# A one-core kernel of three mixer layers: refitted durations, the shared port of two engines, and overwriting transfers in the planner that sets the order of issue

## The chip, the core and the metric

The kernel runs on one core of a Trainium2 chip. A core has five instruction streams: PE (matrix products, with its weight loads as PEld), DVE (VectorE), ACT (ScalarE), POOL (GpSimd) and SP, which here only issues transfers. Each stream works in its own order; semaphores tie them together. The metric is the device time of one execution in microseconds, the median of several runs.

## The reference

Input x is 512 tokens by 1024, all in float32. Two blocks follow each other; the first has an even and an odd layer, the second has one layer. Each layer is a projection of 1024 columns into many, several kinds of attention, a gate, and a projection back.

```python
# first block, two layers
mod = cond @ w_ada[layer] + b_ada[layer]          # cond = silu(c), one row: a matrix-vector product
shift, scale, gate = jnp.split(mod, 3, axis=-1)
h = rmsnorm(x, g_pre[layer]) * (1.0 + scale[:, None, :]) + shift[:, None, :]
...
    y = even_mixer(h, ...)     # z = h @ w_in; MLA attention and sliding-window attention; silu gate; @ w_out
...
    y = odd_mixer(h, ...)      # differential attention and forgetting attention; silu gate; @ w_out
x = x + gate[:, None, :] * rmsnorm(y, g_post[layer])

# second block, one layer
h = x @ w_in
o_nsa = nsa_mixer(...)             # compressed, selected and window attention, gated
o_sb = stick_breaking_mixer(...)
o_hg = hgrn2_mixer(...)            # a gated linear recurrence in chunks of 64
x = layer_norm(ALPHA * x + mixed @ w_out, ln_g, ln_b)
```

## The kernel before, in words

Every float32 product is made of three fp32r products: a value is split into a high part (a cast) and a low part (value less high part). For a weight tile of 128 by 1024 this is `wload`: the transfer into `wraw` (L107), the cast into `whir` on ACT (L109) and the subtraction into `wlor` on DVE or POOL (L113); PE then runs high by high, high by low and low by high (`mm`, L80). Activations are split by `split` (L90 on ACT or L94 on DVE for the high part, L95 on DVE for the low part). `wraw`, `whi` and `wlo` have few buffers each, so a weight's transfer starts when an older one has been split.

The row `mod` is a matrix-vector product of 24 weight tiles a layer (of 128 by 1024 each). It is done on DVE: `gemv_acc` multiplies a tile by a column of `cond` and adds it to a sum `sa` (L175 for the first of eight, L177 for the others). These tiles come through one buffer, `graw` (transfer L157), so the next transfer waits for the step on the tile before. In the first layer the first sums take their tiles through `V` and `og` instead (L660), and the first sum is kept in `pthr`; the inputs x come into `Pr` (L648) and the unit matrix into `ident` (L76), which PE needs for its transposes (L140).

In attention, L367 (`dup`) copies key and query rows between partition halves by transfers inside the core's memory (32 or 64 rows by 512); L383 on DVE adds the mask and takes the row's extreme, L385 on ACT takes the exponential, L395 on POOL normalises, PE transposes (L140), L94 or L90 and L95 split the result.

The code writes instructions in a plain order. At its end `Plan(tc).pin()` gives each of the five engines a fixed order: `duration` gives each instruction a time, a time in which it holds its engine, and a third number (for PE the share of activity, for transfers the bytes); `edges` collects what must wait for what; `schedule` is a list scheduler that walks a model of the five engines, and takes on each engine the ready instruction with the best rank (the place in the plain order, mixed with the longest path that hangs on it, weight `PATH`); `pin` fixes the order that comes out. The real waits are those of the data and of the buffers; the plan only says in which order an engine comes to them. An engine that stands at an instruction whose data isn't there does nothing else.

In the names of rows a number behind a name (`graw_472`) is the instance; in rows of the trace these numbers are left out.

Of the kernel before, what the change touches and what calls it, by code (L numbers as in the profile page):

```python
# [1780 lines left out]
class Plan:  # L1781
# [4 lines left out]

    ENGINES = {"PE": 0, "DVE": 1, "Activation": 2, "Pool": 3, "SP": 4}
    LATENCY = (55, 35, 35, 35, 35)
    BYTES_PER_NS, DMA_LATENCY, LANES = 330.0, 1700.0, 8
    QUANTUM, QUIET, TABLE = 3413.0, 0.6, 1283  # L1790
    PATH = 0.10

    def __init__(self, tc):
        self.tc = tc
# [34 lines left out]
        return t, p0, p1, self.masks[key]  # L1829


    def duration(self, x, e):
        kind = type(x).__name__[4:]
        aps = lambda l: [a.bass_ap for a in l if getattr(a, "bass_ap", None) is not None]
        free = lambda ap: math.prod(int(c) for _, c in list(ap.ap)[1:])
        psum = lambda ap: "PSUM" in str(getattr(ap.tensor, "space", ""))
        I, O = aps(x.ins), aps(x.outs)
        if e == 0:
            n, m = free(I[0]), free(I[1])
            w = 108 if m > 64 else 60  # L1840
            if x.is_transpose:
                return 275, 112, 0
            if "float32r" in str(x.ins[0].dtype):
                n = max(n / 2.26, w if m > 32 else 50)
                return n + 163, n, n
            w = 2 * max(2 * n / 2.26, w if m > 32 else 30)
            return w + 163, w, 4 * n / 2.26 if n > 8 else 0
        if kind == "DMACopy":
            b = 4 * math.prod(int(c) for _, c in O[0].ap)
            return 0, 550 if b <= 140000 else 330, b  # L1850
        if kind == "LoadActFuncSet":
            return self.TABLE, self.TABLE, 0
        n = max(free(a) for a in O + I)
        d = [(int(s), int(c)) for s, c in list(O[0].ap)[1:]]
        rough = n > 64 and (d[-1][0] != 1 or d[-1][1] <= 64 and len(d) > 2)
        if e == 2:
            t = 170 + 0.86 * n + (185 if len(O) > 1 else 0) + (22 if kind == "Activation" and not psum(I[0]) else 0)
            if "Silu" in str(getattr(x, "func", "")):
                t += self.TABLE
            return t, t - 95, 0  # L1860
        if e == 3:
            t = {"Memset": 200 + 0.3 * n, "TensorTensor": (185 + 2.2 * n) * (1.2 if rough else 1),
                 "TensorCopy": 190 + (1.8 if rough else 0.8) * n, "TensorScalarAffineSelect": 290}.get(kind, 290 + 0.76 * n)
            return t, t - 25, 0
        src = bool(I) and psum(I[0])
        wide = sum(free(a) == n for a in I) > 1 or n <= 8
        t = {"Memset": 60 + 0.8 * n, "Reciprocal": 155 + 6.2 * n, "CustomDveAnt": 230 + 1.04 * n, "CopyPredicated": 170 + 1.08 * n,
             "TensorCopy": 150 + (1.05 if src else 0.53) * n,
             "TensorScalarPtr": 150 + (1.1 if wide else 1.05 if src else 0.59) * n}.get(kind, (150 + 1.05 * n) * (1.22 if rough else 1))
        return t, max(t - 80, 120), 0  # L1870

    def edges(self):

# [3 lines left out]
        for i, x in enumerate(self.ins):  # L1877
# [39 lines left out]
    def schedule(self, hard, room, soft):  # L1917

        n = len(self.ins)
# [14 lines left out]
        for i in reversed(order):  # L1934
            d, occ, act = self.cost[i]
            if self.eng[i] == 4:
                d = act / self.BYTES_PER_NS + self.DMA_LATENCY + occ
# [12 lines left out]
        bus, lanes = 0.0, deque([0.0] * self.LANES)  # L1950
        work, slow, told = {}, {}, 0
        for _ in range(n):
            t, e = min((max(free[e], 0.0 if here[e] else coming[e][0][0]), e) for e in range(5) if here[e] or coming[e])
            while coming[e] and coming[e][0][0] <= t:
                i = heapq.heappop(coming[e])[1]
                heapq.heappush(here[e], (rank[i], i))
            i = heapq.heappop(here[e])[1]
            d, occ, act = self.cost[i]
            end = t + d
            if e == 0:  # L1960
                q = int(t / self.QUANTUM)
                while told < q:
                    slow[told + 1] = work.get(told, 0.0) < self.QUIET * self.QUANTUM
                    told += 1
                share = min(1.0, act / occ)
                if slow.get(q):
                    occ *= 2
                end = t + occ + 163
                a = t
                while a < t + occ:  # L1970
# [6 lines left out]
            elif e == 4:  # L1977
                t = max(t, lanes.popleft())
                bus = max(t + occ, bus) + act / self.BYTES_PER_NS
                end = bus + self.DMA_LATENCY  # L1980
                lanes.append(end)
            start[i], free[e] = t, t + occ
            for j, kind in after[i]:
# [171 lines left out]
```

## Time and profile before

| what | value |
|---|---|
| time, median of 3 runs | 1021.7 us (1021.32, 1021.7, 1027.0) |
| the profiled execution's own time | 1020.98 us |
| its span | 1019.3 us |
| mean granted clock of PE | 0.970 |
| PE busy | 929.0 us, 91% |
| DVE busy | 713.8 us, 70% |
| ACT busy | 535.5 us, 53% |
| POOL busy | 246.7 us, 24% |
| moved by transfers | 137.38 MB |

The span is the time from the first to the last instruction that the profile shows; the execution's own time is 1.7 us more. The clock is a mean over the span: 1.00 is PE's full speed (2.4 GHz), and 0.5 its lower level (1.2 GHz). Busy time of PE is modelled for matmuls, which overlap one another.

### The profile page before, as it was taken

Reading aid. Unit: us, or ns where it says so; the run is one execution under the profiler, and the core shown is the slowest. Engines: PE = TensorE matmul, PEld = TensorE weight load, DVE = VectorE, ACT = ScalarE, POOL = GpSimd, SP = SyncE. Lnnn points to the kernel's source line nnn. Section 1 sums busy time; section 2 is a strip of 40 time slices with the busy share of each in tenths; the row PEclk is TensorE's granted clock in tenths of the full one; section 3 lists DMA queues with packets and bytes.
Section 4 is the critical chain, followed back from the end, with each engine's and each line's share of the span. In section 5 each row is a group of like instructions: output and inputs, shape, how many; then the busy total and the mean of one; then the engine's idle time right before and its main releaser. Section 6 shows DMA issues by size and latency. Waiting matters only on the chain.

```text
span 1019.3 us, 14797 instructions
## 1 busy us (share of the span) xinstructions
PE 929.0 (91%) x4999; PEld 768.2 (75%) x4999; DVE 713.8 (70%) x1581; ACT 535.5 (53%) x1180; POOL 246.7 (24%) x274
## 2 busy tenths in 40 slices
PE   3889999868999899999999999999888998999896
PEld 2667887657767787779888778887786877787685
DVE  6886678847987856776466756466799586587737
ACT  6443667628644434575366843553533583575720
POOL 0230123203330011231021420033145134443440
PEclk9899999878999999999999999998999999999999
DMA  9656455366457447651654543333401624431232
GB/s 359 244 157 185 155 118 170 110 150 166 125 188 228 141 132 185 165 135 42 170 143 127 160 132 124 104 115 95 142 22 52 152 53 119 111 107 29 77 123 83
DMA packets 56671, 137.38 MB, mean 135 GB/s; under 512 B 15047, under 2 KB 15431, under 8 KB 56596
## 3 DMA queue, kind: packets, MB, share of 16 engines
q1 hardware_dynamic: 56596, 136.44, 45.8%
q8 instruction: 40, 0.66, 0.3%
q14 instruction: 35, 0.29, 0.1%
HBM read 105.42 MB, written 8.44 MB: 112 GB/s over the span
## 4 chain that ended last, share of the span: by engine, by line
PE 62%; DVE 16%; DMA 10%; ACT 5%; issue 3%; SPq 2%; POOL 2%; DVEq 0%; POOLq 0%; ACTq 0%
PE accr L80 45%; PE sr L80 7%; PE o L80 5%; PE tr L140 4%; DMA graw<-in_w_ada_dram 4%; DMA V<-in_w_ada_dram 2%; DVE wlor L113 2%; DVE sa L177 1%; DMA wrawr<-in_w_ev_dram 1%; DVE ptl L95 1%; DMA qk<-qk 1%; SPq L367 1%; ACT whir L109 1%; DMA tmpr<-tmpr 1%; ACT Pr L385 1%
## 5 line engine op out<-in xcount | busy, mean ns | idle before, releaser
L80 PE MATMUL accr<-hh,whir 128*128 128x512 f32 x516 | 208.5, 404 | 10.0 <-DVE V L95 5.6
L80 PE MATMUL accr<-hl,whir 128*128 128x512 f32 x516 | 207.3, 402 | 1.5 <-DVE hl L690 1.3
L80 PE MATMUL accr<-hh,wlor 128*128 128x512 f32 x516 | 207.8, 403 | 0.0
L109 ACT CAST whir<-wrawr 128x1024 fp32r<-128x1024 f32 (+5 forms) x110 | 111.6, 1015 | 113.3 <-PE accr L80 64.3
L113 DVE TENSOR_TENSOR wlor<-wrawr,whir 128x1024 fp32r<-128x1024 f32 (+6 forms) x93 | 114.1, 1230 | 68.9 <-ACT whir L109 65.0
L395 POOL TENSOR_SCALAR Pr<-Pr,sm 128x256 f32<-128x256 f32 (+2 forms) x120 | 75.9, 649 | 251.4 <-DVE sm L1154 80.8
L80 PE MATMUL accr<-whir,hh 128*128 128x256 f32 (+4 forms) x364 | 119.5, 331 | 4.3 <-ACT whir L109 3.9
L80 PEld LDWEIGHTS accr<-hh,whir 128*128 128x128 f32 x516 | 98.8, 191 | 31.5 <-issue 7.3
L80 PE MATMUL accr<-whir,hl 128*128 128x256 f32 (+4 forms) x364 | 118.2, 328 | 2.2 <-DVE hl L95 2.1
L80 PE MATMUL accr<-wlor,hh 128*128 128x256 f32 (+4 forms) x364 | 119.3, 329 | 0.3 <-DVE wlor L113 0.3
L385 ACT ACTIVATE Pr<-Pr,nm 128x256 f32<-128x256 f32 (+3 forms) x176 | 95.6, 546 | 42.1 <-DVE nm L383 41.5
L80 PEld LDWEIGHTS accr<-hl,whir 128*128 128x128 f32 x516 | 98.9, 192 | 21.1 <-DVE hl L690 2.2
L80 PEld LDWEIGHTS accr<-hh,wlor 128*128 128x128 f32 x516 | 98.5, 191 | 19.4 <-issue 0.7
L80 PE MATMUL sr<-qk,qk 128*128 128x256 f32 (+11 forms) x400 | 93.0, 333 | 6.4 <-DVE nm L383 3.8
L95 DVE TENSOR_TENSOR ptl<-tr,pthr 128x256 fp32r<-128x256 f32 (+3 forms) x160 | 71.8, 464 | 27.1 <-ACT pthr L90 22.6
L140 PE MATMUL tr<-ident,Pr 128*128 128x128 f32 x392 | 72.0, 289 | 12.7 <-DVE ptl L95 6.8
L80 PEld LDWEIGHTS sr<-qk,qk 128*128 128x128 f32 (+2 forms) x400 | 65.7, 192 | 19.4 <-DVE nm L383 7.1
L80 PEld LDWEIGHTS accr<-whir,hh 128*128 128x128 f32 x364 | 70.4, 194 | 11.2 <-ACT whir L109 4.6
L80 PEld LDWEIGHTS accr<-whir,hl 128*128 128x128 f32 x364 | 70.8, 195 | 7.2 <-DVE hl L95 2.8
L80 PEld LDWEIGHTS accr<-wlor,hh 128*128 128x128 f32 x364 | 70.8, 195 | 6.1 <-DVE wlor L113 1.3
L140 PEld LDWEIGHTS tr<-ident,Pr 128*128 128x128 f32 x392 | 48.2, 147 | 28.3 <-issue 10.2
L90 ACT CAST pthr<-tr 128x384 fp32r<-128x384 f32 (+3 forms) x124 | 52.9, 441 | 29.8 <-PE tr L140 28.8
(369 smaller groups left out, 1744.1 us busy)
## 6 DMA issues: line engine op xcount, KB each, us to landing
graw<-in_w_ada_dram SPq DMA_DIRECT2D x32, 512.0 KB
wrawr<-in_w_od_dram SPq DMA_DIRECT2D x30, 512.0 KB
wrawr<-in_w_dram SPq DMA_DIRECT2D x29, 512.0 KB
qk<-qk SPq DMA_DIRECT2D x111, 128.0 KB
wrawr<-in_w_out_dram SPq DMA_DIRECT2D x24, 512.0 KB
wrawr<-in_w_ev_dram SPq DMA_DIRECT2D x17, 512.0 KB
V<-in_w_ada_dram SPq DMA_DIRECT2D x14, 512.0 KB
qk<-tmpr SPq DMA_DIRECT2D x34, 128.0 KB
```

The lines of the kernel that those rows point to most:

```text
L80: self.nc.tensor.matmul(out, a, b, start=start, stop=stop, skip_group_check=True)
L90: self.nc.scalar.copy(hi, src)
L95: self.nc.vector.tensor_tensor(lo, src, hi.bitcast(F32), ALU.subtract)
L109: self.nc.scalar.copy(hi[:, :n], raw[:, :n])
L113: eng.tensor_tensor(lo[:, :n], raw[:, :n], hi[:, :n].bitcast(F32), ALU.subtract)
L140: self.nc.tensor.transpose(out, in_, self.ident[:k, :k])
L177: self.nc.vector.scalar_tensor_tensor(acc, raw, c, acc, ALU.mult, ALU.add)
L367: self.nc.sync.dma_start(dst.bitcast(F32), src.bitcast(F32))
L385: nc.scalar.activation(Pi, Pi, AF.Exp, bias=nm[:, i:i + 1], scale=-1.0, accum_out=s[:, i:i + 1])
L395: self.nc.gpsimd.tensor_scalar(v, v, r[:, i:i + 1], 1.0, ALU.mult, ALU.mult)
```

## The change

Only the planner's model is changed; the instructions and their number stay. Five things differ. Transfers move 410 bytes per ns in the model (330 before) with 1700 ns of latency from SBUF and 2300 from DRAM (1700 before), and SP is held 590, 500 or 330 ns by one (550 or 330 before). Durations of ACT, POOL and DVE forms are refitted. DVE and POOL instructions that use the port which both share (on POOL the tensor-tensor operations) delay each other, and the scheduler takes another ready instruction when the port would make one wait more than 200 ns. A transfer that overwrites rows which an earlier transfer of the same queue still reads is now a true dependence (`< 4`), where before it was only an order. The weight of the longest path goes from 0.10 to 0.16, and the model's threshold for a slow PE from 0.6 to 0.27.

```diff
-    BYTES_PER_NS, DMA_LATENCY, LANES = 330.0, 1700.0, 8
-    QUANTUM, QUIET, TABLE = 3413.0, 0.6, 1283
-    PATH = 0.10
+    BYTES_PER_NS, DMA_LATENCY, LANES = 410.0, (1700.0, 2300.0), 8
+    QUANTUM, QUIET, TABLE = 3413.0, 0.27, 1283
+    PORT, WAIT = 150.0, 200.0
+    PATH = 0.16
...
             b = 4 * math.prod(int(c) for _, c in O[0].ap)
-            return 0, 550 if b <= 140000 else 330, b
+            return self.DMA_LATENCY["DRAM" in str(I[0].tensor.space)], 590 if b <= 70000 else 500 if b <= 140000 else 330, b
...
-            t = 170 + 0.86 * n + (185 if len(O) > 1 else 0) + (22 if kind == "Activation" and not psum(I[0]) else 0)
+            t = 170 + 0.86 * n + (22 if kind == "Activation" and not psum(I[0]) else 0)
             if "Silu" in str(getattr(x, "func", "")):
                 t += self.TABLE
-            return t, t - 95, 0
+            if n <= 8:
+                t += 85
+            elif kind == "Activation" and len(O) == 1 and any(free(a) == 1 for a in I[1:]):
+                t += 100
+            return (t + 90, t + 90, 0) if len(O) > 1 else (t, t - 95, 0)
+        big = [psum(a) for a in I if free(a) > 8]
         if e == 3:
-            t = {"Memset": 200 + 0.3 * n, "TensorTensor": (185 + 2.2 * n) * (1.2 if rough else 1),
+            t = {"Memset": 200 + 0.3 * n, "TensorTensor": (185 + 2.2 * n) * (1.25 if rough else 1.1),
...
-            return t, t - 25, 0
+            return t, t - 25, kind == "TensorTensor"
         src = bool(I) and psum(I[0])
-        wide = sum(free(a) == n for a in I) > 1 or n <= 8
-        t = {"Memset": 60 + 0.8 * n, "Reciprocal": 155 + 6.2 * n, "CustomDveAnt": 230 + 1.04 * n, "CopyPredicated": 170 + 1.08 * n,
+        wide = sum(free(a) == n for a in I) > 1
+        port = big.count(False) > 1 or big == [False] and kind in ("TensorCopy", "TensorScalarPtr")
+        if kind == "CustomDveAnt":
+            return 155 + 1.04 * n, 150 + 1.04 * n, 0
...
-                        same = self.eng[j] == self.eng[i]
+                        same = self.eng[j] == self.eng[i] < 4
...
+            late = lambda i: max(port[4 - e] - self.PORT - t, 0.0) if e in port and self.cost[i][2] else 0.0
             i = heapq.heappop(here[e])[1]
+            if late(i) > self.WAIT:
+                held = [(rank[i], i)]
+                while here[e] and late(here[e][0][1]) > self.WAIT:
+                    held.append(heapq.heappop(here[e]))
+                i = heapq.heappop(here[e])[1] if here[e] else held.pop(0)[1]
...
             d, occ, act = self.cost[i]
+            if e in port:
+                d, occ = d + late(i), occ + late(i)
+                if act:
+                    port[e] = t + d
```

On PE 2797 of 4772 instructions stand at another place than before (6.8 places on average, 71 at most), on DVE 978 of 1581 (2.0 on average), on ACT 492 of 972, on POOL 91 of 277, on SP 274 of 530 (1.5 on average, 36 at most). Three places are shown.

The first is SP's queue at the start of the program. `V`, `og` from `in_w_ada` are the tiles of the first two matrix-vector sums, `Pr` the input x, and `ident` the unit matrix.

```order
+L660 DMA og_16_102<-in_w_ada_dram 128x1024 x2
 L648 DMA Pr0_7_82<-in_x_dram 128x1024
-L660 DMA og_16_102<-in_w_ada_dram 128x1024
 L648 DMA Pr1_8_84<-in_x_dram 128x1024
-L660 DMA og_16_102<-in_w_ada_dram 128x1024
+L660 DMA V_17_107<-in_w_ada_dram 128x1024
 L648 DMA Pr2_9_86<-in_x_dram 128x1024
 L660 DMA V_17_107<-in_w_ada_dram 128x1024
 L648 DMA Pr3_10_88<-in_x_dram 128x1024
-L660 DMA V_17_107<-in_w_ada_dram 128x1024
+L660 DMA V_18_112<-in_w_ada_dram 128x1024 x2
 L76 DMA ident_11_90<-in_ident_dram 128x128
```

Both tiles of `og` now stand ahead of the first input, and both of `V_18` ahead of `ident`, so that twelve loads of 512 KB stand ahead of it where ten did.

The second is DVE where the even layer's latent attention begins (202 to 216 us of the trace). `sa<-graw` is a step of the matrix-vector sum, `V<-accr` the low part of the attention's values, `qk` the rotated queries, `wlor` the low part of a weight. Before:

```order
L95 TENSOR_TENSOR V_415_1984<-accr0_416_1985,V_415_1984 128x4x64
L177 SCALAR_TENSOR_TENSOR sa_435_2087<-graw_458_2171,cond_5_72,sa_435_2087 128x1024
L95 TENSOR_TENSOR V_414_1983<-accr1_417_1996,V_414_1983 128x4x64
...
L95 TENSOR_TENSOR V_415_1984<-accr0_419_2018,V_415_1984 128x4x64
L177 SCALAR_TENSOR_TENSOR sa_435_2087<-graw_472_2230,cond_5_72,sa_435_2087 128x1024
L327 TENSOR_TENSOR qk_426_2053<-accr1_423_2035,qk_425_2052 128x512
L113 TENSOR_TENSOR wlor2_629_2841<-wrawr0_627_2839,whir2_628_2840 128x1024
L327 TENSOR_TENSOR qk_428_2055<-accr2_424_2045,qk_427_2054 128x512
L177 SCALAR_TENSOR_TENSOR sa_435_2087<-graw_502_2349,cond_5_72,sa_435_2087 128x1024
L327 TENSOR_TENSOR qk_443_2115<-accr0_440_2097,qk_442_2114 128x512
```

Now:

```order
L95 TENSOR_TENSOR V_415_1984<-accr0_419_2018,V_415_1984 128x4x64
L327 TENSOR_TENSOR qk_426_2053<-accr1_423_2035,qk_425_2052 128x512
L177 SCALAR_TENSOR_TENSOR sa_435_2087<-graw_458_2171,cond_5_72,sa_435_2087 128x1024
L327 TENSOR_TENSOR qk_428_2055<-accr2_424_2045,qk_427_2054 128x512
L113 TENSOR_TENSOR wlor2_629_2841<-wrawr0_627_2839,whir2_628_2840 128x1024
L327 TENSOR_TENSOR qk_443_2115<-accr0_440_2097,qk_442_2114 128x512
```

The step on `graw_458` has gone behind the splits of `V` and one `qk` (8 places); those on `graw_472` and `graw_502` have left this stretch (39 and 52 places later, among the softmax instructions L383 and L95), and that on `graw_518` stands 8 places later. On SP the transfers of `graw_472` and `graw_502` stand 25 and 36 places later, among the 32-row `dup` transfers.

The third is SP's queue between 85 and 97 us of the trace. `graw` are again matrix-vector tiles, `wrawr` weights of the input projection.

```order
 L157 DMA graw_227_1135<-in_w_ada_dram 128x1024
-L157 DMA graw_231_1144<-in_w_ada_dram 128x1024
 L107 DMA wrawr1_152_774<-in_w_ev_dram 128x576
 L107 DMA wrawr0_187_958<-in_w_ev_dram 128x1024
-L157 DMA graw_245_1213<-in_w_ada_dram 128x1024
+L157 DMA graw_231_1144<-in_w_ada_dram 128x1024
 L107 DMA wrawr1_208_1046<-in_w_ev_dram 128x1024
 L107 DMA wrawr0_228_1138<-in_w_ev_dram 128x1024
+L157 DMA graw_245_1213<-in_w_ada_dram 128x1024
```

Two weights now go ahead of the second `graw`, which waits for the one buffer.

## Rows read from the trace of the kernel before

**Rows 1.** The page: busy time of each engine, and the chain that ended last.

```profile
PE 929.0 (91%) x4999; PEld 768.2 (75%) x4999; DVE 713.8 (70%) x1581; ACT 535.5 (53%) x1180; POOL 246.7 (24%) x274
...
PE 62%; DVE 16%; DMA 10%; ACT 5%; issue 3%; SPq 2%; POOL 2%; DVEq 0%; POOLq 0%; ACTq 0%
```

**Rows 2.** Busy time in stretches: length, PE, PEld, DVE, ACT, POOL, clock, DMA share, GB/s.

```profile
8.00:13.00 5.00, 0.00 (x0) 0.00 (x0) 3.38 (x8) 4.06 (x10) 0.00 (x0) 1.00 1.03 417
...
97.50:101.00 3.50, 3.48 (x16) 3.14 (x15) 2.73 (x7) 2.08 (x6) 0.00 (x0) 0.51 0.80 263
...
204.00:229.50 25.50, 17.33 (x65) 13.69 (x64) 12.58 (x21) 7.54 (x17) 1.05 (x1) 0.80 0.68 149
...
357.00:382.50 25.50, 25.50 (x127) 20.39 (x126) 13.11 (x18) 9.15 (x13) 2.60 (x2) 1.00 0.45 134
```

**Rows 3.** Timeline of DVE: start, us, form, and the idle time before with its releaser.

```profile
207.59 1.28 DVE L177 SCALAR_TENSOR_TENSOR sa<-graw,cond,sa 128x1024 f32<-128x1024 f32 x1 [5.42 <-DMA graw<-in_w_ada_dram]
...
221.76 1.28 DVE L177 SCALAR_TENSOR_TENSOR sa<-graw,cond,sa 128x1024 f32<-128x1024 f32 x1 [3.34 <-DMA graw<-in_w_ada_dram]
...
246.71 1.28 DVE L177 SCALAR_TENSOR_TENSOR sa<-graw,cond,sa 128x1024 f32<-128x1024 f32 x1 [1.99 <-DMA graw<-in_w_ada_dram]
```

**Rows 4.** Timeline of PE: matmuls with long idle time before them, 60 to 250 us.

```profile
72.50 0.74 PE L80 MATMUL accr<-whir,hh 128*128 128x512 f32 x2 [2.18 <-ACT whir L109]
...
97.11 0.54 PE L80 MATMUL accr<-whir,hh 128*128 128x288 f32 x2 [1.74 <-ACT whir L109]
...
210.22 0.77 PE L80 MATMUL accr<-hh,whir 128*128 128x512 f32 x1 [5.64 <-DVE V L95]
...
223.70 0.70 PE L80 MATMUL accr<-hh,whir 128*128 128x512 f32 x1 [2.53 <-DVE qk L327]
...
249.18 1.09 PE L140 MATMUL tr<-ident,Pr 128*128 128x128 f32 x4 [3.60 <-DVE ptl L95]
```

**Rows 5.** Timeline of SP's transfers around them (start, us of issue).

```profile
85.61 5.46 SPq L157 DMA_DIRECT2D graw<-in_w_ada_dram  x2
...
199.34 0.33 SPq L157 DMA_DIRECT2D graw<-in_w_ada_dram  x1
...
214.86 0.33 SPq L157 DMA_DIRECT2D graw<-in_w_ada_dram  x1
...
241.80 0.59 SPq L367 DMA_DIRECT2D qk<-hl  x1
242.44 0.58 SPq L157 DMA_DIRECT2D graw<-in_w_ada_dram  x1
```

**Rows 6.** Timeline of DVE and POOL, instructions under the shared port.

```profile
5.23 0.75 DVE L175 TENSOR_SCALAR pthr<-V,cond 128x1024 f32<-128x1024 f32 x1 [1.46 <-DMA V<-in_w_ada_dram]
...
61.05 3.23 DVE L175 TENSOR_SCALAR sa<-graw,cond 128x1024 f32<-128x1024 f32 x1
...
250.04 1.48 POOL L395 TENSOR_SCALAR Pr<-Pr,sm 128x256 f32<-128x256 f32 x2
...
250.16 0.90 DVE L95 TENSOR_TENSOR qk<-og,qk 128x512 fp32r<-128x512 f32 x1
```

**Rows 7.** Groups by form on DVE: count, then busy us and mean ns of one.

```profile
L95 DVE TENSOR_TENSOR qk<-og,qk 128x512 fp32r<-128x512 f32 x16 | 12.0, 752 | 0.2
```

**Rows 8.** Timeline of PE and DVE at the start, and late in the program (736 to 857 us).

```profile
17.01 0.66 PE L140 MATMUL sr<-ident,Pr 128*128 128x128 f32 x2 [17.01 <-DMA ident<-in_ident_dram]
...
24.98 2.12 DVE L682 SCALAR_TENSOR_TENSOR moda<-modc,gpre 128x4 f32<-128x4 f32 x1
...
738.37 0.71 PE L80 MATMUL tr<-V,tmpr 128*128 128x128 f32 x4 [2.25 <-ACT tmpr L1586]
...
844.91 2.34 DVE L94 CAST Pr<-sa 128x384 fp32r<-128x384 f32 x1
...
847.30 0.44 PE L80 MATMUL tr<-Pr,tri 128*128 128x384 f32 x1 [1.54 <-DVE Pr L94]
...
856.43 0.44 PE L80 MATMUL o<-ptl,V 128*64 128x512 f32 x1 [1.80 <-DVE ptl L95]
```

More of the change, by code (lines that the diff above doesn't have):

```diff
@@ L1843, in duration @@
             if "float32r" in str(x.ins[0].dtype):
-                n = max(n / 2.26, w if m > 32 else 50)
-                return n + 163, n, n
+                w = max(n / 2.26, w if m > 32 else 50)
+                return w + 163, w, n / 2.4 if n >= 32 else 0
             w = 2 * max(2 * n / 2.26, w if m > 32 else 30)
-            return w + 163, w, 4 * n / 2.26 if n > 8 else 0
+            return w + 163, w, n / 1.2 if n >= 32 else 0
         if kind == "DMACopy":
             b = 4 * math.prod(int(c) for _, c in O[0].ap)
-            return 0, 550 if b <= 140000 else 330, b
+            return self.DMA_LATENCY["DRAM" in str(I[0].tensor.space)], 590 if b <= 70000 else 500 if b <= 140000 else 330, b
         if kind == "LoadActFuncSet":
@@ L1856, in duration @@
         if e == 2:
-            t = 170 + 0.86 * n + (185 if len(O) > 1 else 0) + (22 if kind == "Activation" and not psum(I[0]) else 0)
+            t = 170 + 0.86 * n + (22 if kind == "Activation" and not psum(I[0]) else 0)
             if "Silu" in str(getattr(x, "func", "")):
                 t += self.TABLE
-            return t, t - 95, 0
+            if n <= 8:
[4 more added lines that the diff above has]
+        big = [psum(a) for a in I if free(a) > 8]
         if e == 3:
-            t = {"Memset": 200 + 0.3 * n, "TensorTensor": (185 + 2.2 * n) * (1.2 if rough else 1),
+            t = {"Memset": 200 + 0.3 * n, "TensorTensor": (185 + 2.2 * n) * (1.25 if rough else 1.1),
                  "TensorCopy": 190 + (1.8 if rough else 0.8) * n, "TensorScalarAffineSelect": 290}.get(kind, 290 + 0.76 * n)
-            return t, t - 25, 0
+            return t, t - 25, kind == "TensorTensor"
         src = bool(I) and psum(I[0])
-        wide = sum(free(a) == n for a in I) > 1 or n <= 8
-        t = {"Memset": 60 + 0.8 * n, "Reciprocal": 155 + 6.2 * n, "CustomDveAnt": 230 + 1.04 * n, "CopyPredicated": 170 + 1.08 * n,
+        wide = sum(free(a) == n for a in I) > 1
+        port = big.count(False) > 1 or big == [False] and kind in ("TensorCopy", "TensorScalarPtr")
+        if kind == "CustomDveAnt":
+            return 155 + 1.04 * n, 150 + 1.04 * n, 0
+        t = {"Memset": 60 + 0.8 * n, "Reciprocal": 165 + 4 * n, "CopyPredicated": 170 + 1.08 * n,
              "TensorCopy": 150 + (1.05 if src else 0.53) * n,
-             "TensorScalarPtr": 150 + (1.1 if wide else 1.05 if src else 0.59) * n}.get(kind, (150 + 1.05 * n) * (1.22 if rough else 1))
-        return t, max(t - 80, 120), 0
+             "TensorScalarPtr": 205 + 1.1 * n if n <= 8 else 150 + (1.1 if wide else 1.05 if src else 0.59) * n,
+             }.get(kind, 150 + 1.05 * n + (290 if rough else 0))
+        return t, max(t - 80, 120), port
     def edges(self):
@@ L1936, in schedule @@
             if self.eng[i] == 4:
-                d = act / self.BYTES_PER_NS + self.DMA_LATENCY + occ
+                d += act / self.BYTES_PER_NS + occ
             path[i] = max([d] + [path[j] + (occ if k else d + 35) for j, k in after[i]])
@@ L1949, in schedule @@
                 heapq.heappush(coming[self.eng[i]], (0.0, i))
-        bus, lanes = 0.0, deque([0.0] * self.LANES)
+        bus, lanes, port = 0.0, deque([0.0] * self.LANES), {1: 0.0, 3: 0.0}
         work, slow, told = {}, {}, 0
@@ L1956, in schedule @@
                 heapq.heappush(here[e], (rank[i], i))
+            late = lambda i: max(port[4 - e] - self.PORT - t, 0.0) if e in port and self.cost[i][2] else 0.0
             i = heapq.heappop(here[e])[1]
+            if late(i) > self.WAIT:
[3 more added lines that the diff above has]
+                i = heapq.heappop(here[e])[1] if here[e] else held.pop(0)[1]
+                for h in held:
+                    heapq.heappush(here[e], h)
             d, occ, act = self.cost[i]
+            if e in port:
+                d, occ = d + late(i), occ + late(i)
+                if act:
+                    port[e] = t + d
             end = t + d
@@ L1964, in schedule @@
                     told += 1
-                share = min(1.0, act / occ)
                 if slow.get(q):
                     occ *= 2
+                share = act / occ
                 end = t + occ + 163
@@ L1979, in schedule @@
                 bus = max(t + occ, bus) + act / self.BYTES_PER_NS
-                end = bus + self.DMA_LATENCY
+                end = bus + d
                 lanes.append(end)
```

## The prediction

> **What bounds the kernel now.** I read the page first. PE is busy 929.0 of 1019.3 us and carries 62% of the chain that ended last; DVE carries 16%, transfers 10%, ACT 5% [rows 1]. So a new order of the same instructions can only take from PE's idle time, which is 1019.3 - 929.0 = 90.3 us, and from time in which PE runs at its lower clock. The busy table by stretches tells where neither is to be had: from 357 to 382.5 us PE is busy 25.50 of 25.50 us at clock 1.00, while from 204 to 229.5 us it is busy 17.33 us at clock 0.80 [rows 2]. Then I went through PE's timeline for its long idle times, and from each to the engine that ended it. The longest is the start: PE does nothing for 17.01 us, until `ident` has come [rows 8]. The next are 5.64 us at 210.22, 2.53 us at 223.70 and 3.60 us at 249.18, each ended by DVE [rows 4]. DVE itself stands there for a transfer: its in-order queue waits 5.42, 3.34 and 1.99 us at three L177 steps whose tile `graw` hasn't come [rows 3]. These steps feed a row that is needed much later; the instructions behind them feed PE. That is the pattern that a better order can mend. The same pattern is smaller at 72.50 (2.18 us) and 97.11 us (1.74 us), where PE waits for a weight's cast [rows 4], and at 738.37, 847.30 and 856.43 us (2.25, 1.54, 1.80) [rows 8].
>
> **The change part by part.** Nothing is added or removed: no instruction, no byte, no buffer. All costs are in what stands ahead of what.
>
> *A, the stretch 199 to 255 us.* The step on `graw_458` goes behind the splits of `V`, those on `graw_472` and `graw_502` leave the stretch, that on `graw_518` goes 8 places later. With them the three PE gaps lose their cause: 5.64 + 2.53 + 3.60 = 11.8 us at most. What is late next? First the steps themselves. They share one buffer, so a step can't follow another faster than transfer plus step. The transfer issued at 242.44 was used at 246.71 [rows 5, 3], 4.27 us; with the step of 1.28 us that is 5.55 us. In the new order `graw_502` stands 17 and `graw_518` another 13 DVE instructions behind `graw_472`; at DVE's mean of 713.8 / 1581 = 0.45 us [rows 1] that is 7.7 and 5.9 us, just enough. With the slowest transfer there, issued at 199.34 and used at 207.59 (8.25 us) [rows 5, 3], each of the three steps would wait 4 us more, 12 us in all. Between 0 and 12 I take 3, nearer to the fast transfer, since the one at 242.44 was issued in the midst of the `dup` stream, where the new ones will be too. Second, SP: its `dup` transfers go out every 0.64 us (241.80 to 242.44 [rows 5]), and queries and keys come no faster than that, so I leave half of the last gap, 1.8 us. Third, the clock: 0.80 over 25.5 us [rows 2] is 5.1 us of lost full speed; as part of it is the idle time itself, I take back 1.7 us. A = -11.8 + 3 + 1.8 - 1.7 = -8.7 us, bounds -16.9 (both returns nothing, all 5.1 of the clock) and 0.
>
> *B, 60 to 100 us.* Ahead of the matmul of 72.50 about ten matmuls of another sum now stand, which cover its 2.18 us. At 97.11 the weight was queued on SP behind two `graw` transfers that held SP for 5.46 us from 85.61 [rows 5]; the second of them now goes behind that weight. I take 1.2 of the 1.74 us. The clock was 0.51 from 97.5 to 101 us with PE busy 3.48 of 3.50 us [rows 2], which would be 1.7 us more if it doesn't fall. B = -3.4, bounds -5.6 and 0.
>
> *C, the start.* Twelve loads of 512 KB stand ahead of `ident` instead of ten. The loads stream at 417 GB/s between 8 and 13 us [rows 2], so one takes 1.26 us and PE begins 2.5 us later, at about 19.5. ACT also makes a weight's cast ahead of the scaling of the last inputs, another 1.1 to 1.3 us (an estimate from the 1.28 us of an equal tile on DVE [rows 3]). For this the first matrix-vector sum ends sooner, since its tiles come ahead of the inputs, and PE's long wait is not the only thing that the first product needs: `moda` at 24.98 us, which took 2.12 us for four columns [rows 8], is as much on its way. Bounds -2.0 (`moda` no longer stretched, the rest hidden) and +3.8; I take +1.
>
> The Trainium skill, page "DMA: Bandwidth & Descriptors", section "Bandwidth", speaks against the new rate of 410 bytes per ns: it has loads from HBM bound at about 358 GB/s for a core. By that a load would take 1.46 us, PE would begin 2.9 us later, and the forecast would be 0.4 us higher; the 417 GB/s of the trace differ, and decide.
>
> *D, the late gaps.* The three at 738.37, 847.30 and 856.43 sum to 5.6 us. The one at 847.30 comes from a DVE cast of 128x384 at 844.91 that took 2.34 us [rows 8]; a POOL tensor-tensor operation ran beside it, which now stands 4 places earlier. At 738.37 PE has two other sums to do first now. But DVE and ACT have the same chain to do. Half, -2.5; bounds -5.6 and 0.
>
> *The port itself.* A first step of a sum took 0.75 us alone at 5.23 and 3.23 us at 61.05 beside a POOL operation [rows 6]. The new rule would avoid the second, but the two instructions stand in the same order as before there, as at several such places; outside of D and C I give the rule nothing, and it can't cost more than it saves except through E. POOL's L395 are not counted by the rule. An L95 that began at 250.16 while two of them ran took 0.90 us [rows 6] where the mean of its form is 0.752 [rows 7]: 0.15 us.
>
> The Trainium skill, page "SBUF — State Buffer", section "Who interferes with whom", says that a VectorE instruction with two inputs in SBUF is held by any GpSimd instruction that reads SBUF, until that one has ended. The row at 250.16 agrees in kind. The three moved L177 steps read two such tiles and now stand among the L395; by that rule each could grow by one L395 (1.48 / 2 = 0.74 us [rows 6]), 2.2 us in all, and the forecast would be 1010.
>
> *E, everything else.* PE's remaining idle time is 90.3 - 17.0 - 11.8 - 3.9 - 5.6 = 52.0 us in many small gaps, and 2797 of 4772 PE instructions moved. The trace of before can't say which of these gaps close and which open. A tenth of it either way, +5 and -5, taken as 0.
>
> **The sum.** -8.7 - 3.4 + 1 - 2.5 + 0 = -13.6 us on the profiled execution's 1020.98: 1007.4. The median of the runs is 0.7 us above that execution, so I forecast 1008 us. All bounds together would give -35 and +9 us, 986 and 1030.
>
> **The rivals.** *The waits come back.* The steps on `graw_472`, `graw_502` and `graw_518` now stand in DVE's queue amid the softmax, and the instructions behind them feed PE just as the splits of `V` did. If transfers there take 8.25 us and not 4.27, A falls to -1.5; with the rest 1020.98 - 1.5 - 3.4 + 1 - 2.5 = 1014.6, 1015 as a median. For it: those issued at 199.34 and 214.86 were used 8.25 and 6.90 us later [rows 5, 3]. Against it: the gap of 1.99 us at 246.71 was the smallest, in the place that the new ones share.
>
> *The rules don't act where it matters.* The pairs under the port keep their order, as at 61.05, the late gaps stay, and B is only moved on. Then 1020.98 - 8.7 + 1 = 1013.3, 1014 as a median.
>
> *Slower: SP is too late for DVE.* The transfer of `graw_472` stands behind 25 more transfers, most of them `dup`s at 0.64 us, 16 us of SP's time. DVE has 39 instructions to do meanwhile, 39 x 0.45 = 17.6 us. If SP is held by one `dup` that waits for its rows, so that `graw_472` is issued later than 17.6 - 4.3 = 13.3 us after DVE begins on them, DVE stands with the whole attention behind it, and the next two transfers can only start after that step. Three waits of 8.25 us are 24.8 us; less the three removed ones (10.75) that is +14, and with the start at +1 and B at -3.4, 1033 as a median. The new dependence on overwritten rows is in the plan to show such holds to it, which speaks against this rival; that a transfer's true time of 4 to 8 us is still more than the plan's 2.3 us and 1.3 for the bytes speaks for it.
>
> *More.* The gaps close and the clock doesn't fall in A and B: the better bounds of both with the rest as taken, 1020.98 - 16.9 - 5.6 + 1 - 2.5 = 997.
>
> **How the numbers follow.** About 1% is what measurement of this kernel can tell from no change; that is 1011.5 and 1031.9 us. The forecast (1000 to 1011) has 0.41, more 0.13, the waits that come back 0.22, the rules that don't act 0.10, slower 0.14. Faster is the first two and a little of the fourth, 0.55; slower 0.14; the same 0.31. The range leaves out the outer half of "more" and most of "slower": 996 to 1025 us.
>
> **What the new profile would show.** Right: PE's gaps at 210 and 223 us are gone or under 1 us, and the L177 steps on DVE have no idle time over 2 us between 200 and 250 us. PE's first instruction is at 19 to 20 us. The cast of 844.91 takes under 0.5 us. From 357 to 382.5 us nothing differs. Wrong: long idle times before L177 steps among the softmax instructions near 225 to 245 us; or PE's busy time at a lower mean clock than 0.970 for new gaps in stretches that were full; or a first product that begins more than 3 us later.

## The result, and the profile after

The changed kernel takes 997.24 us, the median of four runs (991.52 to 998.21), where the kernel before takes 1023.52 in the same set (1021.32 to 1027.0). The ratio is 0.9729 with a 95% interval of 0.9679 to 0.9778: 2.7% faster, which is 26 us by the two medians and 28 by the ratio, where 13.6 were forecast. The profiled execution has a span of 996.1 us, 23.2 less than before, at a mean clock of 0.977.

The busy times of the changed kernel, against [rows 1]:

```profile
PE 919.3 (92%) x4999; PEld 765.5 (77%) x4999; DVE 711.8 (71%) x1581; ACT 536.0 (54%) x1180; POOL 245.6 (25%) x274
```

The work of the engines is the same. PE's idle time fell from 90.3 to 996.1 - 919.3 = 76.8 us, by 13.5. Its busy time fell by 9.7 us, and most of that is clock: time lost to a lower granted clock (the length of a stretch times what its mean clock lacks to 1.00) is 30.8 us of the span before and 23.1 now, 7.7 less. Where this happened is best seen by counting: the order of PE's matmuls changes little in the large, so the start of the n-th matmul in either trace tells how far each kernel has come. (These are worked out from the traces, row by row. Where the order differs, the same count can hold somewhat other work.)

| PE's matmul | before, us | changed, us | later or earlier |
|---|---|---|---|
| 200th | 57.4 | 63.1 | +5.6 |
| 400th | 105.3 | 103.8 | -1.5 |
| 800th | 178.3 | 181.7 | +3.4 |
| 1200th | 272.1 | 277.5 | +5.4 |
| 3000th | 626.8 | 624.7 | -2.1 |
| 3300th | 687.9 | 686.5 | -1.4 |
| 4000th | 815.8 | 803.2 | -12.6 |
| 4990th | 1008.5 | 985.4 | -23.2 |

Up to two thirds of the program the change gives almost nothing: a loss at the start, a gain from 60 to 104 us, a loss from there to 180 us and a smaller one up to 277, and 7.5 us won back by 625 us (354.7 us from the 1200th to the 3000th matmul before, 347.2 now), for which no experiment was made. All but 1.4 us of the gain comes after 690 us. This is the other way round from the forecast, which had 11.1 of its 13.6 us before 260 us (A, B and C).

The busy table by stretches, first of the changed kernel (columns as in [rows 2]), then the stretch from 728 to 797 us of the kernel before, which stood in no row so far:

```profile
357.00:382.50 25.50, 25.50 (x124) 19.28 (x124) 12.94 (x17) 9.77 (x15) 2.60 (x2) 1.00 0.50 141
...
728.00:797.00 69.00, 67.44 (x454) 57.48 (x454) 60.62 (x117) 31.36 (x56) 31.13 (x35) 1.00 0.32 86
```

```profile
728.00:797.00 69.00, 59.20 (x406) 49.72 (x405) 59.38 (x113) 28.68 (x51) 29.55 (x35) 0.98 0.22 60
```

In most of the time from 728 to 797 us DVE and POOL make the gated recurrence (L1560 to L1683 of the code), a chain in which PE has only small products. DVE is as full in both kernels (59.38 and 60.62 of 69 us), and the chain ends at nearly the same time; its last masked copy (L1660) starts at 789.0 us before, at 790.0 now:

```profile
L1660 DVE COPY_PREDICATED graw<-cs,sr x18: 426/436/451, 712.3 to 789.0; 128x256 f32<-128x256 int32 x18
```

```profile
L1660 DVE COPY_PREDICATED graw<-cs,sr x18: 427/440/448, 710.7 to 790.0; 128x256 f32<-128x256 int32 x18
```

(The numbers are the shortest, median and longest duration in ns, then the first and last start.) But beside this chain PE now does 67.44 us of work instead of 59.20. It is work of the projections, which the kernel before made later. PE's small products of the chain show the other side (count, then busy us and mean ns, then PE's idle time just before them and what ended it; first before, then the changed kernel):

```profile
L80 PE MATMUL sr<-sa,tmpr 128*128 128x128 f32 x96 | 13.3, 283 | 6.4 <-DVE sa L1648 3.8 <-POOL sa L1648 1.6 <-POOL sa L1645 1.0
```

```profile
L80 PE MATMUL sr<-sa,tmpr 128*128 128x128 f32 x96 | 12.8, 276 | 0.3 <-DVE sa L1648 0.3
```

The same 96 products stood behind 6.4 us of waiting for the chain, and now behind 0.3. DVE's timeline in the changed kernel shows what else DVE makes meanwhile, and the line after it when the kernel before made its next such split of a weight:

```profile
755.31 1.65 DVE L113 TENSOR_TENSOR wlor<-wrawr,whir 128x1024 fp32r<-128x1024 f32 x1
756.88 0.77 DVE L1660 COPY_PREDICATED graw<-cs,sr 128x256 f32<-128x256 int32 x2
...
758.56 0.42 DVE L95 TENSOR_TENSOR V<-accr,V 128x256 fp32r<-128x256 f32 x1
758.90 1.32 DVE L113 TENSOR_TENSOR wlor<-wrawr,whir 128x1024 fp32r<-128x1024 f32 x1
```

```profile
765.88 1.22 DVE L113 TENSOR_TENSOR wlor<-wrawr,whir 128x1024 fp32r<-128x1024 f32 x1
```

Between the steps of the chain (L1648, L1660, L1645) stand splits of weights (L113) and of values (L95), which release PE's next products. Before, DVE had nothing but steps of the chain and the splits of values here from 751 to 762 us, and the next weight split came at 765.88; some splits of weights and values stand 15 to 43 places earlier in DVE's order now.

PE's timeline has the gaps that the forecast wanted to see gone, in other places, and a new one at the start (to be read against [rows 4] and [rows 8]):

```profile
19.60 0.66 PE L140 MATMUL sr<-ident,Pr 128*128 128x128 f32 x2 [19.60 <-DMA ident<-in_ident_dram]
...
36.26 0.79 PE L80 MATMUL accr<-hl,whir 128*128 128x512 f32 x1 [4.83 <-DVE hl L690]
...
226.15 0.67 PE L80 MATMUL accr<-hh,whir 128*128 128x512 f32 x1 [2.94 <-DVE qk L327]
...
259.99 0.44 PE L80 MATMUL sr<-qk,qk 96*128 96x128 f32 x2 [3.30 <-DVE nm L383]
```

### The profile page after: what moved, and what is told of

Its sections match the earlier page's. It is cut to its first block, busy times and chain, and to the rows that moved or that the text cites. A ratio compares the mean times of both kernels' runs of the same rounds, so it can differ in the third digit from the quotient of the medians.

```text
span 996.1 us, 14786 instructions
## 1 busy us (share of the span) xinstructions
PE 919.3 (92%) x4999; PEld 765.5 (77%) x4999; DVE 711.8 (71%) x1581; ACT 536.0 (54%) x1180; POOL 245.6 (25%) x274
## 4 chain that ended last, share of the span: by engine, by line
PE 44%; DVE 6%; ACT 3%; DMA 2%; issue 1%; POOL 1%; DVEq 0%; ACTq 0%; SPq 0%; POOLq 0%
PE accr L80 32%; PE sr L80 6%; PE o L80 3%; PE tr L140 2%; DMA wrawr<-in_w_out_dram 1%; DVE wlor L113 1%; DMA qk<-qk 1%; DVE ptl L95 1%; PE tr L80 0%; PE sr L140 0%; DMA wrawr<-in_w_dram 0%; ACT whir L109 0%; DVE graw L1660 0%; DVE tmpr L1635 0%; ACT Pr L385 0%
## 5 line engine op out<-in xcount | busy, mean ns | idle before, releaser
L113 DVE TENSOR_TENSOR wlor<-wrawr,whir 128x1024 fp32r<-128x1024 f32 (+6 forms) x93 | 118.3, 1273 | 63.8 <-ACT whir L109 63.5
L395 POOL TENSOR_SCALAR Pr<-Pr,sm 128x256 f32<-128x256 f32 (+2 forms) x120 | 76.8, 656 | 220.9 <-DVE sm L1154 45.8
L80 PE MATMUL accr<-whir,hh 128*128 128x256 f32 (+4 forms) x364 | 116.0, 325 | 2.9 <-DVE hS L95 1.0
L80 PE MATMUL accr<-whir,hl 128*128 128x256 f32 (+4 forms) x364 | 115.0, 324 | 0.4 <-DVE hl L95 0.3
L80 PE MATMUL accr<-wlor,hh 128*128 128x256 f32 (+4 forms) x364 | 114.2, 322 | 0.9 <-DVE wlor L113 0.9
L80 PE MATMUL sr<-qk,qk 128*128 128x256 f32 (+11 forms) x400 | 95.3, 335 | 11.1 <-DVE nm L383 5.1
L95 DVE TENSOR_TENSOR ptl<-tr,pthr 128x256 fp32r<-128x256 f32 (+3 forms) x160 | 72.4, 464 | 25.0 <-ACT pthr L90 21.5
L140 PE MATMUL tr<-ident,Pr 128*128 128x128 f32 x392 | 75.4, 293 | 11.0 <-DVE ptl L95 5.0
L80 PEld LDWEIGHTS accr<-whir,hl 128*128 128x128 f32 x364 | 68.8, 190 | 5.4 <-DVE hl L95 0.9
L80 PEld LDWEIGHTS accr<-wlor,hh 128*128 128x128 f32 x364 | 68.8, 191 | 5.1 <-DVE wlor L113 1.2
```

The lines of the kernel that those rows point to most:

```text
L80: self.nc.tensor.matmul(out, a, b, start=start, stop=stop, skip_group_check=True)
L95: self.nc.vector.tensor_tensor(lo, src, hi.bitcast(F32), ALU.subtract)
L113: eng.tensor_tensor(lo[:, :n], raw[:, :n], hi[:, :n].bitcast(F32), ALU.subtract)
L140: self.nc.tensor.transpose(out, in_, self.ident[:k, :k])
L395: self.nc.gpsimd.tensor_scalar(v, v, r[:, i:i + 1], 1.0, ALU.mult, ALU.mult)
```

## The experiments

"Late part" below is the time from PE's 3000th to its 4990th matmul in the profiled execution, counted as above: 381.7 us before, 360.7 in the changed kernel. "Early part" is up to the 3000th: 626.8 and 624.7. A single profile has an uncertainty of some microseconds: a second trace of the changed kernel (e12 below) has 355.6 and 621.8.

**Which part of the change makes the gain.** The first two kernels take the shared port out of the changed planner, and put it alone into that of before.

```diff
# e1, on the changed kernel
-            late = lambda i: max(port[4 - e] - self.PORT - t, 0.0) if e in port and self.cost[i][2] else 0.0
+            late = lambda i: max(port[4 - e] - self.PORT - t, 0.0) if False else 0.0
# e2: the changed kernel's schedule() with the durations, transfer model, path weight,
# PE's clock model and dependences of before
```

> The changed planner without the shared port (neither its time nor the choosing of another instruction); all refitted durations, the transfer model, the path weight and the new dependence stay. Theory P (the port rule makes the gain, which lies from 725 us on): PE loses the work that filled its idle time in the recurrence, the time is 1013 to 1023 us and PE's timeline has its long gaps near 738 and 780 us again. Rival D (the refitted durations and the transfer model make it): 993 to 1003 us.

Measured: 1028.12 us, ratio 1.0042 (1.0009 to 1.0075). All other parts of the change together make the kernel slightly slower, and above the range of theory P. Among them is one that the account of the change doesn't list: with the model's threshold for a slow PE, also what the model counts as PE's work was changed.

> The planner of before with the port alone (its time and the choosing); durations, transfer model, path weight and dependences as before. Theory P: most of the gain is there, 996 to 1006 us, and without the loss at the start, since the loads keep their order (PE begins at 17 us). Rival D: 1013 to 1023 us.

Measured: 1009.57 us, ratio 0.9869 (0.9814 to 0.9924): half of the gain, which neither theory had. By parts it is plain: the late part is 362.4 us, 19.3 less than before and nearly all of the gain there; the early part is 633.2, 6.4 more. In e1 the late part is 375.7 and the early one 639.3. So the port rule makes nearly all of the late gain, alone. What it loses early is gone in the changed kernel, though the other parts alone lose 12.5 us there; why the two are good together is not shown.

**Is the place right?** The next kernel has two orders in one (`Old` is the planner of before).

```diff
-        start = self.schedule(hard, room, soft)
+        one, two = Old(self.tc), self
+        start = one.schedule(*one.edges())
+        then = two.schedule(*two.edges())
+        cut = sorted(start[i] for i in range(len(start)) if self.eng[i] == 0)[3000]
+        start = [s if s < cut else 1e9 + t for s, t in zip(start, then)]
```

> Both orders in one kernel: up to PE's instruction 3000 (about 640 us) every engine has the order of before, from there on that of the changed kernel. If the traces tell rightly where the time came from (the same PE instruction 1.3 us earlier at 720 us, 23.2 us earlier at the end), this has all but 1 or 2 us of the gain: 997 to 1001 us. If the gain needs the early part too (its loads or its clock): over 1008 us.

Measured: 1000.12 us, ratio 0.9776 (0.9715 to 0.9837). As expected: the order after PE's 3000th instruction makes the gain, with the old order ahead of it.

**What of the port rule it is.** The rule does two things: it lets the model's DVE and POOL take longer, and it lets the scheduler take another instruction.

```diff
# e3: the time alone
-    PORT, WAIT = 150.0, 200.0
+    PORT, WAIT = 150.0, 1e9
# e10: the choosing alone
-            if e in port:
-                d, occ = d + late(i), occ + late(i)
-                if act:
-                    port[e] = t + d
+            if e in port and act:
+                port[e] = t + d
```

> The changed planner, in which the port still delays DVE and POOL in the model, but the scheduler never takes another instruction for it. If it is enough that the plan knows how long DVE needs, PE's other work is still drawn forward: 994 to 1002 us. If choosing another instruction is what counts: 1008 to 1020 us. The DVE time above the medians of the forms was 38.0 us before and 41.9 us after, so that the choosing avoids collisions is doubtful already.

Measured: 1016.58 us (four runs from 1006.06 to 1021.45), ratio 0.9896 (0.9815 to 0.9977), late part 376.9.

> The changed planner, in which the port makes the scheduler take another instruction, but never adds time to one in the model. Theory N: PE's order doesn't know of the slow chain, its idle time from 728 to 797 us stays at 7 to 10 us and the time is 1012 to 1026 us. If choosing alone is the gain: 996 to 1004 us.

Measured: 1024.14 us, ratio 1.0014 (0.9982 to 1.0046), late part 371.6 (the early part is 635.9). Neither alone gives the late part of 360.7. The busy rows of the recurrence show both short of it (e3 first, then e10, which comes to the recurrence 11 us after the changed kernel, so that its stretch is moved on by 12):

```profile
728.00:797.00 69.00, 63.88 (x426) 54.41 (x426) 57.39 (x113) 30.18 (x53) 29.53 (x35) 0.95 0.20 57
```

```profile
740.00:809.00 69.00, 59.91 (x385) 50.43 (x385) 56.27 (x109) 26.70 (x49) 31.58 (x34) 0.98 0.27 73
```

In e3 the plan counts more time for the recurrence, but DVE takes the steps of the chain first: three splits of weights that the changed kernel makes amid the chain (755 to 765 us) come after its last step (790 to 798 us), and PE makes few other products beside the chain (the count stands in the table below). In e10 DVE makes splits sooner, but PE's order stays near to that of before and has PE wait for the chain.

**Without the rule, by rank.** Is it the collisions that the choosing avoids, or the splits that it draws ahead? Two kernels draw the splits ahead by their rank, on the planner of before (e5) and on that of e3 (e9).

```diff
         for i, x in enumerate(self.ins):
             if type(x).__name__ == "InstLoadActFuncSet":
                 rank[i] = -2.0
+            if i > 0.6 * n and self.eng[i] == 1 and any(w and t.name.startswith(("wlo", "V_")) for w, t, *_ in self.acc[i]):
+                rank[i] -= 0.08
```

> The planner of before, without port rule or refits; only the rank of DVE's splits of weights (wlo) and values (V) from 60% of the program on is better, so that DVE takes them sooner between the steps of the recurrence (the V splits 25, 15 and 2 places earlier, two wlo splits 18 and 12; the changed kernel has them 30, 25, 16 and 33, 29 earlier). Theory M (the gain from 725 to 800 us comes from splits that release PE and are drawn ahead into DVE's full stretch, collisions or not): PE's idle time from 728 to 797 us falls from 9.8 to 4 to 7 us and the time is 4 to 8 us below the kernel before. Rival (DVE bounds the stretch, and what is drawn ahead only lengthens its chain): no gain, or up to 4 us slower.

Measured: 1017.25 us, ratio 0.9954 (0.9927 to 0.998). The time is as theory M had it, the place is not: PE's busy time in the recurrence is 58.99 of 69 us, as before, and what it won came after 800 us (815.5 us at the 4000th matmul against 815.8, 1005.0 at the 4990th against 1008.5). (3.5 us less in one profile is within what single profiles differ by.) Theory M in that form fell; drawing the splits ahead is not enough there while PE's order waits for the chain.

> The planner of e3 (the port's time is known, nothing is chosen for it) with the rank of e5 (DVE's splits of weights and values ahead from 60% of the program on). Theory N (two things are needed together: PE's order must know that the recurrence on DVE is slow, and DVE must make the splits between its steps, so that PE has something to do): PE's idle time from 728 to 797 us is under 3 us, as in the changed kernel (1.6) and unlike e3 (5.1) and e5 (10.0), and the time is 993 to 1002 us. If the choosing counts for what it avoids on the port: 1008 to 1018 us, like e3.

Measured: 998.42 us, ratio 0.9785 (0.9753 to 0.9818), late part 362.2. Without any choosing for the port the late gain is back. PE's idle time in the recurrence, however, is more than expected:

```profile
728.00:797.00 69.00, 63.76 (x403) 54.07 (x403) 56.88 (x112) 27.42 (x47) 27.74 (x33) 0.95 0.31 86
```

5.2 us and not under 3, as much as in e3; its two gaps are at 784 and 788 us, later than those of e3, and the way from the 3300th to the 4000th matmul takes 119.5 us (before 127.9, changed 116.7, e3 129.7). So PE's idle time in that stretch does not tell e9 from e3. A count does: how many matmuls of projections (`accr`) PE starts between the first and the last masked copy of the chain (worked out from the traces, row by row).

| kernel | chain, us | projection matmuls in it | PE idle in it, us | lost to a lower clock in it, us | late part, us |
|---|---|---|---|---|---|
| before | 95.3 | 299 | 9.8 | 4.0 | 381.7 |
| e1, no port rule | 94.6 | 308 | 10.0 | 1.7 | 375.7 |
| e3, its time alone | 94.8 | 311 | 5.3 | 6.3 | 376.9 |
| e5, splits ahead by rank | 99.2 | 313 | 10.0 | 4.1 | 378.6 |
| e10, its choosing alone | 96.3 | 321 | 9.4 | 1.7 | 371.6 |
| e2, port rule alone | 93.6 | 344 | 3.0 | 0.0 | 362.4 |
| e9, time and rank | 99.8 | 356 | 5.6 | 2.5 | 362.2 |
| changed | 98.5 | 360 | 1.9 | 2.9 | 360.7 |

The chain takes 94 to 100 us in all of them. Time alone, choosing alone and rank alone bring 12 to 22 more projection matmuls into it, time with one of the others 45 to 61, and the late part by and large follows that count. The 61 of the changed kernel are all of 512 columns; where PE is full they start 0.23 us apart (215.04, 215.27, 215.50 us), so they are worth some 14 us by estimate, two thirds of the late gain. The clock has a share too: 8.5 of the 16.2 us by which e3's late part is longer than the changed kernel's are time lost to a lower clock (12.0 us against 3.4). One of its falls, at 755 us, stands amid PE's gaps of 1.39 and 1.69 us (753.25, 756.07); what brought the others is not shown.

The collisions don't fall in any of these: DVE's time above the median of each form (excesses over 120 ns, worked out from all its rows) is some 38 us before and 41 to 46 in the changed kernel, e3, e9 and e10, by how the forms are grouped.

**Part A, the waits for matrix-vector tiles.**

```diff
             for k in range(8):
-                self.gemv_acc(acc, self.wada(layer, k, part * 1024), k, self.GE)
+                if k == 0:
+                    raw = self.wada(layer, k, part * 1024)
+                self.gemv_acc(acc, raw, k, self.GE)
                 yield
```

> The changed kernel, in which each matrix-vector sum through graw loads one weight tile and uses it for all eight steps: 28 of 32 transfers of 512 KB are left out (the row is then another), the steps stay. DVE's waits for graw (8.7 us between 190 and 260 us, 2 us before) go. If these waits are what kept part A of the prediction from its gain: PE's gaps at 219, 226, 243, 251 and 260 us (11.4 us) shrink to under 4, and the time is 985 to 990 us. If PE is held there by the chain of queries, keys and values: 993 to 998 us.

Measured: 992.33 us, ratio 0.9694 (0.9656 to 0.9732). The time is between the two, and its interval overlaps that of the changed kernel. The trace tells why: from PE's 800th to its 1100th matmul the kernel takes 64.9 us, the changed one 73.5 and the one before 74.7. It is 8.6 us ahead of the changed one there (5.0 of PE's idle time, 3.5 of clock). The planner made a new order for it, so not all of that need be the waits. Then this order runs into a wait for a `dup` transfer, as SP stood 10.89 us at four of them from 234.04 us, and by the 1200th matmul the lead is gone:

```profile
254.85 0.44 PE L80 MATMUL sr<-qk,qk 96*128 96x128 f32 x1 [12.90 <-DMA qk<-hh]
```

So the kernel bears out that the waits for `graw` held PE, as the prediction read them, and the next thing late was SP.

**The start and the path weight.** e6 is the splice of e4 with the cut at PE's instruction 150 instead of 3000; e8 sets `PATH` back to 0.10.

> The changed kernel, with the order of before on every engine up to PE's instruction 150 (some 52 us). The changed kernel is 5.4 us behind at 40 to 60 us, and about level at 100. If what it lost at the start is lost for good: 990 to 993 us. If it catches up from 60 to 100 us because something else sets that stretch: 995 to 999 us.

Measured: 991.06 us, ratio 0.9708 (0.9661 to 0.9756). PE starts at 17.18 us, the 200th matmul comes at 57.3 us (changed 63.1), and the lead is still there later: 616.4 us at the 3000th against 624.7.

> The changed kernel with the path weight of before (0.10). PE's order differs from the changed one by 11 places in the stretch from 800 to 920 us. If the port rule alone makes the late gain: 994 to 1001 us. If it needs the path weight: 1004 to 1015 us. At the start ident goes one load earlier, PE begins near 18.3 us.

Measured: 1000.46 us, ratio 0.9789 (0.9753 to 0.9824). PE began at 16.85 us, not at 18.3. The late part is 365.2: most of the gain is there without the path weight. It is 4.5 us longer than the changed kernel's, 1.7 of them clock, which one profiled execution can't settle.

**The splice beside the changed kernel**, six runs each on one chip.

> The kernel of e6 once more, beside the changed kernel on the same chip, to tell 0.6% apart: 5 to 7 us less than it, if the loss at the start is lost for good, as the spans said (984.3 against 996.1, of which 4 to 6 at the start).

> The changed kernel as it is, for the comparison: 0.97 to 0.976 of the kernel before.

Measured: 988.92 us with a ratio of 0.9679 (0.9642 to 0.9715), and 991.59 us with 0.9717 (0.9681 to 0.9754). The kernel with the old start came out 2.7 us below the changed one, not 5 to 7, and the intervals overlap. In this pair of traces the lead does not stay: 4.3 us at the 200th matmul (57.1 against 61.4), 2.4 at the 3000th and 0.4 at the 4990th (976.9 against 977.3). That it beats the kernel before is plain; that it beats the changed one is not settled.

## Why the prediction was wrong

The direction was right, and the size was not: 13.6 us forecast, 26 to 28 measured, and from another place. That PE's idle time fell by 13.5 us, nearly the figure of the forecast, is chance: the forecast was made of other stretches, and 1.7 us of it were clock. Step by step:

- **The port itself.** "Outside of D and C I give the rule nothing" is the step that failed. I asked what the rule does to the collisions, found the colliding pairs in the same order at 61.05, and stopped. The collisions indeed stayed. What the rule changed is what the plan believes of DVE's speed in the recurrence, together with what DVE does meanwhile. By e3, e5, e9 and e10 neither is enough alone: only with both does PE make 45 to 61 more projection matmuls beside the chain. That goes with some 20 us in the late part (e2: 19.3, changed kernel: 21.0, of which 14.2 are PE's idle time and 3.4 clock).
- **E, everything else**, taken as 0 within 5 us either way, therefore missed the recurrence: 127.9 to 116.7 us from the 3300th to the 4000th matmul. D named only 2.25 us of PE's waits there; PE's idle time from 728 to 797 us was 69 - 59.20 = 9.8 us in many small gaps, which a busy table of that stretch shows.
- **A**, forecast at -8.7: from the 800th to the 1200th matmul the time went from 93.7 to 95.8 us, +2.1, with 18.4 us of PE's idle time before and 19.2 now (the rest is clock and other work in the count). The three gaps of 11.8 us went, and five of 11.4 us came, at 219.51, 226.15, 243.06, 250.94 and 259.99 us. The term that was mis-sized is the return of the waits, "between 0 and 12 I take 3, nearer to the fast transfer". The rows of the changed kernel, SP's issues and DVE's steps:

```profile
207.47 0.33 SPq L157 DMA_DIRECT2D graw<-in_w_ada_dram  x1
...
250.62 0.33 SPq L157 DMA_DIRECT2D graw<-in_w_ada_dram  x1
```

```profile
217.57 1.28 DVE L177 SCALAR_TENSOR_TENSOR sa<-graw,cond,sa 128x1024 f32<-128x1024 f32 x1 [2.86 <-DMA graw<-in_w_ada_dram]
...
258.18 1.28 DVE L177 SCALAR_TENSOR_TENSOR sa<-graw,cond,sa 128x1024 f32<-128x1024 f32 x1 [3.77 <-DMA graw<-in_w_ada_dram]
```

  From issue to use it is 10.1 and 7.6 us in these two, as slow as the slow ones of before, and 4.7 and 4.0 us in the two between them; DVE waits 8.7 us in the four steps, where the sum had 3. The rival "the waits come back" happened: PE's gaps of 1.56, 1.89, 1.66 and 3.30 us stand right behind these four steps. (By the prediction's own terms that rival had A at +0.3, not at -1.5: it left out the 1.8 us kept for SP.) The fifth gap, 2.94 us at 226.15, has another cause, a weight's cast that came late, and no term of the prediction has it:

```profile
224.27 1.23 DVE L113 TENSOR_TENSOR wlor<-wrawr,whir 128x1024 fp32r<-128x1024 f32 x1 [3.08 <-ACT whir L109]
```

  That the waits cost PE time in this stretch is borne out by e7.
- **B**, forecast at -3.4: from the 200th to the 400th matmul 47.9 us before, 40.8 now, -7.1, and 41.5 in e6, which hasn't lost anything before. Right in kind, and twice the size; my bound was 5.6. Half of it is PE's idle time (4.2 us before, 0.8 now: the forecast's gaps), half the clock (3.4 us lost before, none now). But 4.9 us are lost again from the 400th to the 800th matmul (73.0 us before, 77.9 now), 2.8 of them idle time, so that 2.2 are left by then: in good part B was moved on, as the second rival had it.
- **C**, forecast at +1, bound 3.8: +5.6 at the 200th matmul (+4.0 in e12's trace). The later `ident` was right (PE begins at 19.60, as said, 2.6 us later). What I left out stands on DVE, in the changed kernel:

```profile
32.38 3.10 DVE L177 SCALAR_TENSOR_TENSOR sa<-V,cond,sa 128x1024 f32<-128x1024 f32 x1 [1.58 <-DMA V<-in_w_ada_dram]
35.40 0.15 DVE L185 TENSOR_TENSOR modc<-o,bada 128x4 f32<-128x4 f32 x1
```

  A step that waits for a tile now stands ahead of the second half of `modc` and `moda`; before, that half of `moda` came at 30.68 us, and the step behind it. Now the step waits 1.58 us and is then held beside a POOL split to 3.10 us, and PE waits 4.83 us at 36.26. It is the pattern of A, which I had looked for at 207 us and not at the start, though the order shows it. e6 shows that the loss is the start's own.
- **D**, forecast at -2.5: of its three gaps, 5.6 us, 0.37 are left at 738.47 and under 0.3 at each of the others. Right in sign, twice the size. After the recurrence the way from the 4000th to the 4990th matmul went from 192.8 to 182.2 us, 6.4 of it PE's idle time (11.6 to 5.3 us), more than these gaps held. The cast that took 2.34 us at 844.91 now takes 0.35, at 833.89, as said. Of the gap at 957.71 (3.21 us before, the chain of a Silu) 1.44 are left, at 954.71; no term had it.
- **L395 and the moved steps.** The four L177 steps between 215 and 262 us took 1283 to 1286 ns each, so none was held by a POOL operation; the 2.2 us that I had estimated by a rule of the Trainium skill (page "SBUF — State Buffer", section "Who interferes with whom") didn't come up, since none met an L395 there.
- Where nothing was to change, from 357 to 382.5 us, nothing did: PE is busy 25.50 of 25.50 us again.

What stays open: why the port rule's order is 6 us worse in the early part (e2) and the other parts 12 us worse (e1), and good together. From the 1200th to the 3000th matmul, where the changed kernel wins 7.5 us, both take 354.0 us, hardly less than before. No run takes these two apart.

## What to carry to other kernels

Look where an engine that is not the bottleneck is full, and ask what the bottleneck does beside it: here DVE's recurrence was the stretch in which PE's idle time could be filled, and the busy table of that stretch told of it (9.8 us idle), while the longest single waits told of gains that came back elsewhere. Here the port rule in the planner's cost model paid without any fewer collisions: it paid where the plan knew of the slow chain and at the same time the filling work's own preparation was drawn ahead on the full engine. Either alone was worth little in the late part. When a wait is moved, follow the moved instruction to what now stands behind it, at every place where the order shows it.

## What the runs showed of the hardware

Two executions of the changed kernel differ by 8 us in span (996.1 and 988.1) without any instruction in another order. One place can be named, 3.4 of the 8 us: from 690 to 697.5 us the granted clock was 0.54 in the first, mostly its lower level of 1.2 GHz, and 1.00 in the second, and PE had 21 matmuls or 42, being busy all the time in both, there and in the 20 us ahead of it:

```profile
690.00:697.50 7.50, 7.50 (x21) 4.67 (x22) 6.08 (x13) 2.98 (x5) 3.71 (x5) 0.54 0.36 118
```

```profile
690.00:697.50 7.50, 7.50 (x42) 6.49 (x41) 6.72 (x13) 1.70 (x4) 4.77 (x8) 1.00 0.68 216
```

The kernel before had 0.60 there. A full PE in the busy table can thus be a PE at half speed, and single profiles can differ by this much; the parts above of a few microseconds have that uncertainty.
